# Two of four modulation blocks of the expert layer's norm summed on TensorE instead of VectorE

## The chip, the core and the metric

One core of one Trainium2 chip runs the whole program in one launch. The metric is device time in microseconds (us). TensorE (PE) multiplies matrices, VectorE (DVE) and ScalarE (ACT) work elementwise, GpSimd (POOL) as well, and SyncE (SP) issues transfers. Each engine takes its instructions in order and waits on semaphores.

## The reference, cut to what matters

Two models run one after the other on 256 tokens of width 2048. The first block is

```
mod = silu(c) @ w_ada + b_ada                      # (2048) @ (2048 x 12288)
sh1, sc1, ga1, sh2, sc2, ga2 = split(mod, 6)
h = rmsnorm(x, g_mix) * (1 + sc1) + sh1
x = x + ga1 * hybrid_mixer(h)                      # attention and linear recurrence, then @ w_out
h = rmsnorm(x, g_ffn) * (1 + sc2) + sh2
x = x + ga2 * peer(h)                              # the expert layer
```

and the second model has a state-space layer and an attention layer, each with such a modulation of its own. All is float32. The change touches how `mod` is computed for sh2 and sc2, the modulation of the expert layer's norm.

## The kernel before

A projection goes through tiles of weights: `half` transfers 128 x 1024 weights on SP's queue into `raw`, ScalarE rounds them to `wh` (L352), VectorE subtracts to get the rest `wl` (L354), and TensorE multiplies both by the activations `xs` (L365, L366). Every load calls `tick`, which also advances background work at a rate set per stage.

`mod` is such background work. Its 12288 columns are 12 blocks of 1024: 0 to 3 are sh1 and sc1, 4 and 5 ga1, 6 and 7 sh2, 8 and 9 sc2, 10 and 11 ga2. A block is a vector times 2048 x 1024 weights, in 16 chunks of 128 x 1024 that ScalarE's queue transfers into three buffers `graw` (L281). Two ways exist. With an accumulator (`self.gp` is a pool, as in the whole mixer), VectorE multiplies the first chunk by its 128 factors (L317), adds 15 more (L319) into `gacc`, and TensorE then sums gacc over the partitions with a column of ones (L299), in four column groups of the bank `pg`. Without one (blocks 0 to 3 at the start, 10 and 11 in the expert layer), TensorE takes each chunk itself at L299, four fp32 matmuls with the factors as 32 equal stationary columns, and sums in `pg`. In both, ScalarE copies `pg` (L334), TensorE transposes the copy (L339), and VectorE adds the bias (L341).

There is one bank `pg` and one tile `gacc`. A block is written as a generator: one step for a chunk, then for an accumulator one step each for the sum of columns, the copy and the transposes. The steps of the last chunk, of the sum and of the copy yield PAUSE, which ends a load's share:

```
while self.owed >= 1 and self.bg and self.bg[0][0] != self.hold:
    self.owed -= 1
    if self.advance() == PAUSE:
        break
```

In the mixer the order of loads is w_q, w_k, w_f, w_v (1.5 steps a load), w_lx, w_ly (3 steps a load), then w_out, at a pace that lets the blocks 6 to 9 ("ffn") end within 14 loads (`pace("ffn", 14)`); what is left is done behind the last load (`need("ffn")`). By this count block 6 belongs to the lx loads and the first ly loads, block 7 to the ly loads, block 8 to loads 3 to 8 of w_out, and block 9 to loads 11 to 15 and behind.

Each engine's queue is not simply in the order of the program: the framework orders it by the program's order among what its own model takes for ready, so work may be pulled ahead.

The mixer ends with two norms, of the attention half and of the recurrent half: sums of squares (L441, L445, L451), the reciprocal root (L458 to L471, twelve short VectorE operations in a chain), and per tile L479, L481, L482, which write `xs`. w_out's first five tiles run their first halves on the attention half and their second halves on the recurrent half. The residual is L430. The expert layer's norm comes next (`rstd` again, then L479, L484, L485).

Of the kernel before, what the change touches and what calls it, by code (L numbers as in the profile page):

```python
# [9 lines left out]
F = mybir.dt.float32  # L10
# [138 lines left out]
class K:  # L149
# [131 lines left out]
            self.nc.scalar.dma_start(raw, src)  # L281
            self.ahead.append(raw)

    def gemv(self, w, blocks, which, bias, out, big=False):
        nc = self.nc
        if not big:
            self.chunks += [w[128 * k:128 * k + 128, 1024 * b:1024 * b + 1024] for b in blocks for k in range(KD)]
        return self._gemv(w, blocks, which, bias, out, big)

    def _gemv(self, w, blocks, which, bias, out, big):  # L290
        nc = self.nc
        for b in blocks:
            pg = self.pg()[:, :T]
            c0 = slice(1024 * b, 1024 * b + 1024)
            acc = None if big or self.gp is None else self.gp.tile([128, 1024], F, name="gacc", tag="gacc", bufs=1)

            def columns(lhs, m, start, stop):
                for j in range(4):
                    nc.tensor.matmul(pg[32 * j:32 * j + 32, :], lhs, m[:, T * j:T * j + T], start=start, stop=stop,  # L299
                                     skip_group_check=True, tile_position=(0, 32 * j))  # L300

            for k in range(KD):
                if not big:
                    while not self.ahead:
                        self.fetch_chunk()
                    raw = self.ahead.pop(0)
                else:
                    if k % 4 == 0:
                        rt = self.xs(F).rearrange("p a b t -> p (a b t)").rearrange("p (a c) -> p a c", a=4)
                        self.loads.append(  # L310
                            nc.sync.dma_start(rt, w[128 * k:128 * k + 512, c0].rearrange("(a p) c -> p a c", a=4)))
                    raw = rt[:, k % 4]
                ck = self.cact[:, 16 * which + k:16 * which + k + 1]
                if acc is None:
                    columns(ck.to_broadcast([128, 32]), raw, k == 0, k == KD - 1)
                elif k == 0:
                    nc.vector.tensor_scalar(acc, raw, ck, None, op0=OP.mult)  # L317
                else:
                    nc.vector.scalar_tensor_tensor(acc, raw, ck, acc, op0=OP.mult, op1=OP.add)  # L319
                if not big:  # L320
                    while len(self.ahead) < DEEP and self.chunks:
                        self.fetch_chunk()
                if k < KD - 1:
                    yield True


            if acc is not None:
                if not big:
                    yield PAUSE
                columns(self.ones[:, :32], acc, True, True)  # L330
            if not big:
                yield PAUSE
            ev = self.s1()
            nc.scalar.copy(ev, pg)  # L334
            if not big:
                yield PAUSE
            pm = self.pm()
            for h in range(2):
                nc.tensor.transpose(pm[:, 128 * h:128 * h + 128], ev[:, 128 * h:128 * h + 128], self.ident)  # L339
            v = lambda m: m[:, 8 * b:8 * b + 8].rearrange("p (j h) -> p h j", h=2)  # L340
            nc.vector.tensor_add(v(out), pm[:, :T].rearrange("p (h r) -> p h r", h=2)[:, :, 0:128:32], v(bias))  # L341
            yield False
# [229 lines left out]
    def _mixer(self, x):  # L572
        nc, A, sb, cp = self.nc, self.A, self.sb, self.cp
        mod, hs = self.mod, self.hs
        bias = self.col("b_ada", 0, 96)
        self.use_pool(self.ph if GP[0] else None)
        for n, b in (("ga1", (4, 5)), ("ffn", range(6, 10)), ("ga2", (10, 11))):
            self.bg.append([n, self.gemv(A["w_ada"], b, 0, bias, mod), 19 * len(b) + 1])
        for n, w, nb in (("m0", "mod_w0", 6), ("mkv", "kv_mod_w", 4), ("m1", "mod_w1", 6)):
            t = cp.tile([128, 8 * nb], F, name=n)  # L580
            setattr(self, n, t)
# [1083 lines left out]
```

## Time and profile before

| | |
|---|---|
| median of 3 runs | 3511.92 us (3503.63 to 3515.0) |
| the profiled execution | 3513.32 us, span 3511.6 us |
| TensorE busy | 3220.8 us, 92% of the span |
| VectorE busy | 2688.9 us, 77% |
| ScalarE busy | 1675.5 us, 48% |
| VectorE, multiply-adds of L319 | 429.7 us in 315 instructions, mean 1364 ns |
| TensorE, L299 | 36.8 us in the start, 29.7 us on graw, 14.2 us on gacc |

The mixer runs from about 118 to 552 us of the span. Times in the timelines are from the span's start. "idle before" and a bracket with an arrow name what ended an idle time. A busy TensorE is not TensorE at its peak: matmuls overlap and their ends are modelled.

### The profile page before, as it was taken

How to read it: one execution, taken by the hardware profiler on the slowest of the kernel's cores; microseconds unless marked ns; L12 is line 12 of the kernel's file. 1: busy time of each engine (PE TensorE's matmuls, PEld its weight loads, DVE VectorE, ACT ScalarE, POOL GpSimd, SP SyncE). 2: the span in 40 equal slices, each digit the busy share in tenths (PEclk: the TensorE clock that was granted, in tenths of full speed). 3: DMA queues.
4: the chain of work that ended last, by engine and by line, in shares of the span. 5: the costliest groups of instructions: out<-in, count | busy, mean ns of one | idle time of the engine just before them, and what ended most of it. 6: DMA issues, size and time to landing. Idle time of an engine off the chain costs nothing.

```text
span 3511.6 us, 50080 instructions
## 1 busy us (share of the span) xinstructions
PE 3220.8 (92%) x18190; PEld 2684.6 (76%) x18190; DVE 2688.9 (77%) x4213; ACT 1675.5 (48%) x2785; POOL 841.4 (24%) x750
## 2 busy tenths in 40 slices
PE   5889778999989999999999999988889799999998
PEld 3777667788867878778888778767778688888887
DVE  6778878997668888897777787599996756666665
ACT  3436434456545555444444443455445335555553
POOL 1000211145412212112222630235442120222221
PEclk8999889999989999999999999989999899999999
DMA  9995666567788888888788988545466655444443
GB/s 392 336 344 204 217 235 236 176 238 274 259 279 299 296 278 292 298 287 300 267 289 279 320 298 287 178 146 169 141 219 212 208 194 196 157 149 157 153 145 135
DMA packets 263431, 837.68 MB, mean 239 GB/s; under 512 B 26384, under 2 KB 69520, under 8 KB 260112
## 3 DMA queue, kind: packets, MB, share of 16 engines
q1 hardware_dynamic: 198512, 604.69, 49.9%
q10 hardware_dynamic: 64672, 229.80, 18.0%
q8 instruction: 143, 2.34, 0.3%
q14 instruction: 104, 0.85, 0.1%
HBM read 799.66 MB, written 33.69 MB: 237 GB/s over the span
## 4 chain that ended last, share of the span: by engine, by line
PE 60%; DVE 16%; DMA 12%; issue 5%; POOL 4%; ACT 2%; ACTq 0%; DVEq 0%; SPq 0%; POOLq 0%
PE p L365 25%; PE p L366 13%; DVE wl L354 6%; PE pm L948 5%; PE pm L949 5%; PE pm L950 5%; DMA graw<-mod_w 4%; DVE gacc L319 3%; DMA graw<-w_ada 3%; PE pm L902 1%; DMA graw<-kv_mod_w 1%; DVE xs L1329 1%; PE pg L299 1%; POOL t L929 1%; ACT wh L352 1%
## 5 line engine op out<-in xcount | busy, mean ns | idle before, releaser
L365 PE MATMUL p<-xs,wh 128*128 128x512 f32 x5600 | 2040.0, 406 | 86.5 <-DVE xs L485 44.1
L366 PE MATMUL p<-xs,wl 128*128 128x256 f32 x5600 | 1597.2, 285 | 36.7 <-DVE wl L354 36.4
L354 DVE TENSOR_TENSOR wl<-raw,wh 128x1024 fp32r<-128x1024 f32 x996 | 1262.5, 1274 | 454.7 <-ACT wh L352 452.8
L352 ACT CAST wh<-raw 128x1024 fp32r<-128x1024 f32 x996 | 1039.3, 1049 | 945.8 <-PE p L365 379.1
L365 PEld LDWEIGHTS p<-xs,wh 128*128 128x128 f32 x5600 | 1072.4, 192 | 354.0 <-issue 53.3
L366 PEld LDWEIGHTS p<-xs,wl 128*128 128x128 f32 x5600 | 1077.3, 192 | 60.7 <-DVE wl L354 51.3
L319 DVE SCALAR_TENSOR_TENSOR gacc<-graw,cact,gacc 128x1024 f32<-128x1024 f32 x315 | 429.7, 1364 | 106.1 <-DMA graw<-mod_w 52.9
L949 PE MATMUL pm<-wl,xs 128*128 128x512 f32 x1024 | 400.1, 391 | 4.1 <-DVE wl L354 4.1
L948 PE MATMUL pm<-wh,xs 128*128 128x512 f32 x1024 | 401.8, 392 | 0.5 <-DVE x L958 0.5
L950 PE MATMUL pm<-wh,xs 128*128 128x512 f32 x1024 | 399.0, 390 | 0.0
L933 POOL TENSOR_TENSOR xs<-t,xs 128x256 fp32r<-128x256 f32 x128 | 164.5, 1318 | 715.6 <-ACT xs L931 715.6
L949 PEld LDWEIGHTS pm<-wl,xs 128*128 128x128 f32 x1024 | 192.3, 188 | 46.9 <-DVE wl L354 8.6
L948 PEld LDWEIGHTS pm<-wh,xs 128*128 128x128 f32 x1024 | 192.2, 188 | 45.7 <-issue 6.3
L950 PEld LDWEIGHTS pm<-wh,xs 128*128 128x128 f32 x1024 | 192.2, 188 | 40.0
L929 POOL TENSOR_TENSOR t<-t,t 128x256 f32<-128x256 f32 x128 | 158.6, 1275 | 154.6 <-DMA t<-wd 150.5
L445 POOL TENSOR_TENSOR ssq<-ssq,s 128x256 f32<-128x256 f32 x96 | 101.9, 1071 | 367.1 <-ACT s L441 366.1
L918 ACT ACTIVATE t<-et 128x256 f32<-128x256 f32 x128 | 53.7, 420 | 253.6 <-DVE et L422 249.7
L421 ACT COPY et<-p 128x256 f32<-128x256 f32 x281 | 102.8, 367 | 82.2 <-PE p L366 77.6
L892 POOL TENSOR_SCALAR xs<-iof,eT,eT 128x128 f32<-128x128 f32 x64 | 104.2, 1637 | 110.4 <-PE pm L902 76.7
L1578 POOL TENSOR_SCALAR t<-t,st 128x128 f32<-128x128 f32 (+1 forms) x64 | 78.5, 1239 | 127.4 <-DVE st L1576 124.3
L422 DVE TENSOR_TENSOR et<-p,et 128x256 f32<-128x256 f32 x224 | 92.7, 414 | 10.7 <-ACT et L421 10.7
L1329 DVE TENSOR_TENSOR_SCAN xs<-rho,xs 128x128 f32<-128x128 f32 x128 | 80.0, 678 | 4.3 <-POOL xs L1320 4.3
(388 smaller groups left out, 2872.4 us busy)
## 6 DMA issues: line engine op xcount, KB each, us to landing
raw<-peer_u SPq DMA_DIRECT2D x256, 512.0 KB, 5.6
raw<-peer_v SPq DMA_DIRECT2D x256, 512.0 KB, 4.9
graw<-mod_w ACTq DMA_DIRECT2D x192, 512.0 KB, 6.2
graw<-w_ada ACTq DMA_DIRECT2D x128, 512.0 KB, 5.7
raw<-nsa_z SPq DMA_DIRECT2D x96, 512.0 KB, 3.7
xs<-w_ada SPq DMA_DIRECT2D x16, 2048.0 KB, 13.6
graw<-kv_mod_w ACTq DMA_DIRECT2D x64, 512.0 KB, 6.2
raw<-w_out SPq DMA_DIRECT2D x32, 512.0 KB, 4.8
```

Of the source, the lines that this page charges most:

```text
L319: nc.vector.scalar_tensor_tensor(acc, raw, ck, acc, op0=OP.mult, op1=OP.add)
L352: nc.scalar.copy(h, s)
L354: nc.vector.tensor_sub(l, s, h.bitcast(F))
L365: self.nc.tensor.matmul(p, h[:, sl], x, start=k == 0, stop=False, skip_group_check=True)
L366: self.nc.tensor.matmul(p[:, 1], l[:, sl], x[:, 0], start=False, stop=k == KD - 1, skip_group_check=True)
L892: (nc.gpsimd if j == 3 else nc.vector).tensor_scalar(o[:, 1, j], self.iof, eT[1][:, t + j:t + j + 1], eT[2][:, t + j:t + j + 1], op0=OP.is ...
L929: nc.gpsimd.tensor_mul(gc, gc, wv[:, c])
L933: nc.gpsimd.tensor_sub(ap[:, c - 2, 1], gs[:, c - 2], ap[:, c - 2, 0].bitcast(F))
L948: nc.tensor.matmul(pp[t], ah, h[:, sl], start=c == 0, stop=False, skip_group_check=True)
L949: nc.tensor.matmul(pp[t], ah, l[:, sl], start=False, stop=False, skip_group_check=True)
L950: nc.tensor.matmul(pp[t], ap[:, c, 1, 128 * t:128 * t + 128], h[:, sl], start=False, stop=c == 7, skip_group_check=True)
L1329: nc.vector.tensor_tensor_scan(ma[:, j, i], self.rho[:, g:g + 1].to_broadcast([128, 128]), ma[:, j, i], initial=0.0, op0=OP.mult, op1=OP.add)
```

## The change

`gemv` takes a list `pe` of blocks that get no accumulator. The three calls for w_ada in the mixer pass (6, 8). So blocks 6 and 8, the first half of sh2 and the first half of sc2, go chunk by chunk through L299 on TensorE in the mixer; blocks 4, 5, 7 and 9 stay with VectorE, and 10 and 11 are as before.

```
-    def gemv(self, w, blocks, which, bias, out, big=False):
+    def gemv(self, w, blocks, which, bias, out, big=False, pe=()):
...
-        return self._gemv(w, blocks, which, bias, out, big)
+        return self._gemv(w, blocks, which, bias, out, big, pe)
...
-            acc = None if big or self.gp is None else self.gp.tile([128, 1024], F, name="gacc", tag="gacc", bufs=1)
+            acc = None if big or self.gp is None or b in pe else self.gp.tile([128, 1024], F, name="gacc", tag="gacc", bufs=1)
...
         for n, b in (("ga1", (4, 5)), ("ffn", range(6, 10)), ("ga2", (10, 11))):
-            self.bg.append([n, self.gemv(A["w_ada"], b, 0, bias, mod), 19 * len(b) + 1])
+            self.bg.append([n, self.gemv(A["w_ada"], b, 0, bias, mod, pe=(6, 8)), 19 * len(b) + 1])
```

## Rows read from the trace of the kernel before

**Rows 1.** The page, busy time of each engine.
```profile
PE 3220.8 (92%) x18190; PEld 2684.6 (76%) x18190; DVE 2688.9 (77%) x4213; ACT 1675.5 (48%) x2785; POOL 841.4 (24%) x750
```
**Rows 2.** Busy time by stretch: length, engines, PE clock, DMA share, GB/s.
```profile
268.00:345.00 77.00, 71.28 (x386) 61.28 (x386) 65.67 (x139) 47.47 (x107) 7.02 (x14) 0.96 0.58 205
345.00:422.00 77.00, 56.96 (x288) 45.63 (x287) 64.18 (x112) 36.57 (x76) 14.16 (x11) 0.87 0.61 214
422.00:464.00 42.00, 16.88 (x84) 14.13 (x84) 36.82 (x56) 10.00 (x19) 3.99 (x2) 0.70 0.75 257
464.00:504.00 40.00, 39.96 (x218) 34.37 (x218) 26.63 (x41) 18.16 (x27) 8.23 (x7) 0.93 0.41 147
```
**Rows 3.** Timeline of TensorE, 440 to 465 and 544 to 556: start, length, instruction.
```profile
464.04 0.80 PE L365 MATMUL p<-xs,wh 128*128 128x512 f32 x1 [23.62 <-DVE xs L482]
...
547.90 0.86 PE L299 MATMUL pg<-gacc,ones 128*32 128x256 f32 x8 [3.76 <-DVE gacc L319]
...
552.21 1.06 PE L451 MATMUL pm<-ssq,ones 128*128 128x256 f32 x2
```
**Rows 4.** Timeline of VectorE, 425 to 463.
```profile
426.72 1.27 DVE L319 SCALAR_TENSOR_TENSOR gacc<-graw,cact,gacc 128x1024 f32<-128x1024 f32 x1
...
437.86 2.68 DVE L319 SCALAR_TENSOR_TENSOR gacc<-graw,cact,gacc 128x1024 f32<-128x1024 f32 x2
...
441.59 0.42 DVE L458 TENSOR_SCALAR s<-pm 128x256 f32<-128x256 f32 x1
...
443.70 1.22 DVE L354 TENSOR_TENSOR wl<-raw,wh 128x1024 fp32r<-128x1024 f32 x1
...
461.44 0.42 DVE L471 SCALAR_TENSOR_TENSOR rstd<-s,rstd 128x256 f32<-128x256 f32 x1
```
**Rows 5.** Timeline of VectorE, 542 to 560.
```profile
554.23 0.42 DVE L458 TENSOR_SCALAR s<-pm 128x256 f32<-128x256 f32 x1 [1.40 <-PE pm L451]
...
559.16 0.42 DVE L471 SCALAR_TENSOR_TENSOR rstd<-s,rstd 128x256 f32<-128x256 f32 x1
```
**Rows 6.** Busy time by stretch, L319 alone: one stretch for each block 6 to 9.
```profile
243.00:292.00 49.00, 19.02 (x15) 0.97 0.90 321
349.00:407.00 58.00, 19.70 (x15) 0.88 0.60 209
418.00:462.00 44.00, 19.22 (x15) 0.70 0.76 269
504.00:548.00 44.00, 20.72 (x15) 1.00 0.94 335
```
**Rows 7.** Timelines of ScalarE and TensorE at the bank pg.
```profile
291.30 0.35 ACT L334 COPY s<-pg 128x256 f32<-128x256 f32 x1
...
406.97 0.64 PE L299 MATMUL pg<-gacc,ones 128*32 128x256 f32 x8 [1.15 <-DVE gacc L319]
...
466.52 0.37 ACT L334 COPY s<-pg 128x256 f32<-128x256 f32 x1
```
**Rows 8.** Timeline of TensorE in the next stage, one chunk and three chunks.
```profile
706.42 0.28 PE L366 MATMUL p<-xs,wl 128*128 128x256 f32 x1
...
707.20 0.50 PE L365 MATMUL p<-xs,wh 128*128 128x512 f32 x1
...
992.79 0.28 PE L366 MATMUL p<-xs,wl 128*128 128x256 f32 x1
993.00 1.50 PE L299 MATMUL pg<-graw,cact 128*32 128x256 f32 x24
994.43 0.50 PE L365 MATMUL p<-xs,wh 128*128 128x512 f32 x1
```
**Rows 9.** Who waited for whom, 200 to 345: total us, times, longest.
```profile
DVE gacc L319 <- DMA graw<-w_ada: 14.6, 10, 3.1
PE pm L750 <- DVE sl L744: 2.9, 2, 2.6
```
**Rows 10.** Who waited for whom, 430 to 470.
```profile
DVE gacc L319 <- DMA graw<-w_ada: 3.6, 5, 1.0
```

More of the change, by code (lines that the diff above doesn't have):

```diff
@@ L287, in gemv, with _gemv @@
             self.chunks += [w[128 * k:128 * k + 128, 1024 * b:1024 * b + 1024] for b in blocks for k in range(KD)]
-        return self._gemv(w, blocks, which, bias, out, big)
-    def _gemv(self, w, blocks, which, bias, out, big):
+        return self._gemv(w, blocks, which, bias, out, big, pe)
+    def _gemv(self, w, blocks, which, bias, out, big, pe):
         nc = self.nc
```

## Prediction

> **What bounds the kernel now.** I read the totals first, then the stretches of the mixer, then TensorE's longest waits there, then VectorE's timeline at the longest.
>
> TensorE is the busiest engine of the whole run, VectorE second [rows 1]. That average hides the place of this change. In the stretches of the mixer [rows 2] TensorE is nearly full while the lx columns run (71.28 of 77 us from 268 to 345) and full in the first part of the output projection (39.96 of 40 us from 464 to 504). Between them it is not: it idles 20.0 us of the 77 from 345 to 422, and 25.1 us of the 42 from 422 to 464, where VectorE is busy for 36.82 us. The reader is to see that a microsecond of work costs TensorE a microsecond in the first two stretches, and that VectorE sets the pace in the other two.
>
> The 25 us are nearly all one wait: TensorE stands 23.62 us, until 464.04, for the second half of the mixer's normed rows (xs, L482) [rows 3]. VectorE's timeline shows why [rows 4]. The reciprocal root that comes ahead of L482 takes from 441.59 (L458) to 461.86 us (last L471), 20.3 us, because its twelve short operations alternate with the 1.28 us multiply-adds of block 8 (L319). The same chain ahead of the expert layer, with nothing between, takes from 554.23 to 559.58 us, 5.35 us [rows 5]. All 15 multiply-adds of block 8 fall between 418 and 462, where they cost 19.22 us [rows 6]. In the program they belong to the projection's loads 3 to 8: the framework has pulled them ahead into what it took for VectorE's free time.
>
> **The change, part by part.**
>
> *Removed from VectorE:* the 15 multiply-adds of block 6 between 243 and 292, 19.02 us, and those of block 8, 19.22 us [rows 6]; the first multiply of each block is not counted. Also removed, from TensorE: one sum of columns over gacc per block, 0.64 us [rows 7].
>
> *Added to TensorE:* 16 chunks a block, each four fp32 matmuls of 128x32 with 256 columns (eight records). The trace has them in the next stage. One chunk alone moves the next L365 from 0.12 us after the last L366 (an estimate from the steps where nothing stands between) to 0.78 us (706.42 to 707.20): 0.66 us. Three together move it to 1.64 us (992.79 to 994.43): 1.52 us [rows 8]. At three steps a load, block 6 comes as two, four threes, two, and block 8 as five threes and one: 8.3 us each, taking a pair as 1.09. Less 0.64 for the sum that goes, 7.7 us each. Bounds: 16 times 0.51 less 0.64, 7.5; 16 times 0.66 less 0.64, 9.9.
>
> The Trainium skill (TensorEngine Tiling (Array Packing), Tiling Modes, Key Properties) says that a change of tiling mode drains TensorE. The rows agree in that a lone chunk costs 0.66 and one in company 0.51. If every chunk came alone, the two blocks would cost 19.8 us by that, not 15.4.
>
> *Where block 6 goes.* Its columns need the bank pg. That is free only when ScalarE has copied block 5's sum out, at 291.30 [rows 7], while the multiply-adds of before had a tile of their own and ran from 243. So the columns run in the lx stretch, where TensorE has little idle time: +7.7. What VectorE gains there is worth little: of the waits from 200 to 345, 2.9 us are TensorE's for an attention head's softmax (L744) [rows 9]; I take 2 back (bounds 0 and 2.9). TensorE now stands in order for each chunk's transfer. VectorE stood 14.6 us for them in that stretch [rows 9], for block 5 as well and where the DMA was fuller; the bounds are 0 and 7.3, half of it. I take 1, since the DMA share is only 0.58 from 268 on [rows 2]. Block 6: +6.7.
>
> *Where block 8 goes.* For the same reason it waits for the copy of block 7's sum. Before, that sum is made at 406.97, yet ScalarE copies it only at 466.52, among the casts of the norm [rows 7]. So block 8's columns come behind that norm, in the full stretch: +7.7. Waits for chunks: VectorE stood 3.6 us for them [rows 10]; between 0 and 3.6 I take 2. What is queued behind such a wait on TensorE is the next projection tile, and behind a late release of a graw buffer ScalarE's next chunk transfer, which ScalarE issues in order ahead of its casts.
>
> *What it frees.* In the chain from 441.59 there remain 5.35 us [rows 5] and one 1.22 us subtraction of wl that stands there too [rows 4]: 6.6 instead of 20.3, so -13.7. Ahead of it, from 426.72 to 440.54, six more multiply-adds (first and last in [rows 4], 7.7 us) stand between the last tile's gelu and L458: -7.7. Together -21.4, within the wait of 23.62; TensorE ends the five first halves at 440.4 and would go on about 2 us later. What is late next is then the norm itself, as before. Bounds: 13.7 and 23.6.
>
> *Pacing.* A block on TensorE has one step fewer, a pause that ends a load's share. By counting the steps, block 7 moves one load ahead, and block 9 two: its last chunk goes from behind the last load to the second last. In the stretch with 20.0 us of idle I take 2 for block 7's earlier end (bounds 0 and 10). At the mixer's end TensorE is done at 544.14, waits 3.76 us for block 9's last chunk, makes its sum, and begins the sum of squares at 552.21 [rows 3]. Without block 9 in the way some 2 us are left of these 8.1 (last residual, square): up to -6. I take 4, since block 9 now follows block 8 through the same three buffers (bounds 0 and 6).
>
> *Nothing else.* Blocks 4, 5, 10 and 11 are not in (6, 8); bytes, transfers and copies stay the same in number. SP's queue is not touched. The accumulator is free of 6 and 8, which alone would let 7 and 9 begin sooner.
>
> **The sum:** 6.7 + 7.7 + 2 - 21.4 - 2 - 4 = -11.0 us against the profiled execution's 3513.3, which makes 3502.3. That execution is 1.4 us above the median of 3511.9 (runs from 3503.6 to 3515.0), so the median comes to 3501.
>
> **The rivals.**
>
> *More comes back (3487).* The 20.0 us of idle from 345 to 422 are VectorE's doing too, which is busy for 64.18 us there [rows 2]. If block 7, a load earlier, frees half of them (-10 instead of -2), the tail gives its 6 and the chunk waits are 0, the sum is -11 - 8 - 2 - 3 = -24: about 3487. Against: block 7 itself stays with VectorE in that very stretch.
>
> *The waits move along (3509).* TensorE takes over VectorE's waits for chunks, 7.3 and 3.6 instead of 1 and 2: +7.9, so 3509. For it: an in-order queue either way. Against: the DMA share is lower where the columns now run, 0.58 and 0.41 [rows 2].
>
> *The chunk stream becomes the bound (3533).* Blocks 8 and 9, 32 chunks, must now both follow the copy of block 7's sum, through three buffers. I place that copy at 447 (466.5 less 21.4, and some 2 for the norm) and add 7 for block 6: 454. At block 9's pace of before, 2.75 us a chunk (16 in 44 us), they end at 542, sooner than the sum at 547.90 of before; at block 7's pace, 3.6 us (16 in 58 us) [rows 6], at 569, 21 us later: 3533. It decides from 2.9 us a chunk up. For it: before, block 8 had run ahead during the wait. Against: only 147 GB/s are drawn from 464 to 504 [rows 2], so the new transfers have room. This is the rival that ends slower.
>
> *Full price, nothing back (3527).* If other work fills VectorE's chain, the wait stays and the columns cost 15.4: 3527. The candidate is block 9, whose accumulator is free; against it, its chunks queue behind block 8's, which wait for the copy. The Trainium skill (Perfetto Trace Analysis, Identifying the Most-Contended Engine) says to improve the engine with the highest occupancy first; by that, loading TensorE [rows 1] is wrong, where the stretches have VectorE as the busy one from 422 to 464 [rows 2].
>
> That the change does nothing is excluded: the mixer has a pool, so both blocks had an accumulator before.
>
> **How the numbers follow.** About 0.3%, 10.5 us, is what a measurement of this kernel can tell from no change. Forecast 0.36, its centre just at that bound (0.19 faster, 0.17 same); more comes back 0.26; waits move along 0.19; stream 0.13; full price 0.06. So faster 0.45, same 0.36, slower 0.19. The range runs from 3483, below the largest gain, to 3527, the full price; what it leaves out is the slow stream and a little below. The likeliest case's own range is 3494 to 3509.
>
> **What would show it.** Right: L458 to the last L471 of the mixer's second norm in 7 us or less, TensorE's wait for L482 under 5 us, block 6's columns after ScalarE's copy of block 5 and block 8's after that of block 7, 8 to 10 us of displacement each, the sum of squares within 3 us of the last matmul on w_out. Wrong: multiply-adds of block 9 inside that chain, TensorE idle ahead of L299 for graw by more than 5 us, block 9's last chunk still behind the last load, or block 8's columns found inside the old wait.

## The result, and the profile after

The changed kernel takes 3531.76 us (median of five runs, 3527.28 to 3538.18), the kernel before beside it 3511.01 us: a ratio of 1.0061, with a 95% interval of [1.0048, 1.0074]. It is 0.6% slower, where 3501 us was forecast. The profiled execution took 3527.28 us, with a span of 3525.6 us.

The page's busy times, which answer to [rows 1]:

```profile
PE 3246.7 (92%) x18430; PEld 2696.4 (76%) x18430; DVE 2653.8 (75%) x4181; ACT 1681.4 (48%) x2789; POOL 847.3 (24%) x750
```

VectorE has 35 us less to do and TensorE 26 us more; the page says no more than that. The stretches of [rows 2], with the projection's second part as a fifth row:

```profile
268.00:345.00 77.00, 74.28 (x476) 57.18 (x475) 51.95 (x115) 42.94 (x97) 6.66 (x13) 0.98 0.63 207
345.00:422.00 77.00, 57.13 (x269) 46.28 (x267) 55.11 (x87) 35.38 (x72) 15.98 (x11) 0.84 0.62 206
422.00:464.00 42.00, 29.04 (x153) 23.32 (x152) 35.97 (x79) 17.56 (x34) 1.74 (x2) 0.84 0.41 134
464.00:504.00 40.00, 37.30 (x270) 27.42 (x269) 17.66 (x23) 12.64 (x17) 4.41 (x5) 1.00 0.83 293
504.00:552.00 48.00, 42.71 (x235) 35.40 (x234) 42.28 (x47) 18.66 (x24) 10.50 (x8) 1.00 0.94 343
```

From 422 to 464 TensorE has 29.04 us of work in place of 16.88: the gap ahead of the projection is smaller. From 345 to 422 it still idles 19.9 us, although VectorE has 9 us less to do there. And from 464 to 504 the DMA share is 0.83, where it was 0.41: block 8's chunks now come beside the projection's weights.

TensorE's timeline, which answers to [rows 3] and to the bank's rows in [rows 7]: the first and last columns of block 6, block 7's sum, the second norm, the first and last columns of block 8, block 9's sum, the end of w_out.

```profile
289.08 1.07 PE L299 MATMUL pg<-graw,cact 128*32 128x256 f32 x16
...
344.11 0.63 PE L299 MATMUL pg<-graw,cact 128*32 128x256 f32 x6
...
414.54 1.08 PE L299 MATMUL pg<-gacc,ones 128*32 128x256 f32 x8 [5.46 <-DVE gacc L319]
...
457.67 0.79 PE L365 MATMUL p<-xs,wh 128*128 128x512 f32 x1 [6.72 <-DVE xs L482]
...
462.10 1.50 PE L299 MATMUL pg<-graw,cact 128*32 128x256 f32 x24
...
500.27 0.64 PE L299 MATMUL pg<-graw,cact 128*32 128x256 f32 x8
...
544.79 0.62 PE L299 MATMUL pg<-gacc,ones 128*32 128x256 f32 x2
...
559.97 0.28 PE L366 MATMUL p<-xs,wl 128*128 128x256 f32 x1
...
562.39 0.60 PE L451 MATMUL pm<-ssq,ones 128*128 128x256 f32 x2
```

VectorE's chain of the second norm, which answers to [rows 4]:

```profile
449.65 0.42 DVE L458 TENSOR_SCALAR s<-pm 128x256 f32<-128x256 f32 x1
...
452.03 1.22 DVE L354 TENSOR_TENSOR wl<-raw,wh 128x1024 fp32r<-128x1024 f32 x1
...
455.46 0.43 DVE L471 SCALAR_TENSOR_TENSOR rstd<-s,rstd 128x256 f32<-128x256 f32 x1
```

The chain takes 6.2 us in place of 20.3, with the one subtraction of wl that was left in it, and TensorE's wait for L482 is 6.72 us in place of 23.62. The step that the prediction put most on is as it said. But the wait ends at 457.67, only 6.4 us sooner than before, because all ahead of it is late: block 7's sum is made at 414.54 behind a wait of 5.46 us, where it was made at 406.97 behind 1.15 [rows 7].

Matching the matmuls of the weights (L365) one by one gives how far each trace is behind that of before, in us, at the places where before stood at these times. A row is the first matmul of an output tile, the last one the first of the next stage. The columns behind the first two are experiments told below; the last of them has the same program as before up to 562 us, so that its column shows what chance does to such a number: up to 6 us to its level, but at most 1.5 from one row to the next.

```
before at   the change   pauses kept   block 6's columns left out   same mixer
   316         -0.3         -1.7                1.8                    -4.7
   328          8.6          7.2                2.3                    -6.2
   363         15.8          0.2                2.3                    -4.9
   405         18.5          1.6              -10.3                    -3.8
   431         13.2          0.1              -12.7                    -4.3
   470         -1.2        -16.2              -29.9                    -2.9
   498          8.6         -3.9              -10.6                    -3.2
   538         16.0         -3.4               -3.8                    -3.5
   562          9.3         -5.0               -9.6                    -4.4
```

Read down the changed kernel's column (in steps from row to row): +9 while block 6's columns end in lx (expected, 6.7), 5 to 10 more in ly (a gain of 2 was expected), a large gain at the norm, +10 for block 8's columns (expected, 7.7 and 2), another 7 in the projection's second part (not expected), and back some 7 at the end (4 was expected). The mixer ends 9 us late. The two profiled executions differ by 14.0 us and the medians by 21, so that by the medians about 12 more are lost behind it, where the prediction had nothing; the experiments below test that.

### The profile page after: what moved, and what is told of

The parts are those of the page before. It is cut to its first block, busy times and chain, and to the rows that moved or that the text cites. A ratio compares the mean times of both kernels' runs of the same rounds, so it can differ in the third digit from the quotient of the medians.

```text
span 3525.6 us, 50448 instructions
## 1 busy us (share of the span) xinstructions
PE 3246.7 (92%) x18430; PEld 2696.4 (76%) x18430; DVE 2653.8 (75%) x4181; ACT 1681.4 (48%) x2789; POOL 847.3 (24%) x750
## 4 chain that ended last, share of the span: by engine, by line
PE 60%; DVE 17%; DMA 12%; issue 6%; POOL 2%; ACT 2%; ACTq 0%; DVEq 0%; SPq 0%; POOLq 0%
PE p L365 24%; PE p L366 12%; DVE wl L354 6%; PE pm L948 5%; PE pm L950 5%; PE pm L949 5%; DMA graw<-mod_w 4%; DVE gacc L319 3%; DMA graw<-w_ada 2%; DMA graw<-kv_mod_w 2%; PE pm L902 1%; PE pg L299 1%; DMA s5d<-tb 1%; DVE xs L1329 1%; ACT wh L352 1%
## 5 line engine op out<-in xcount | busy, mean ns | idle before, releaser
L365 PE MATMUL p<-xs,wh 128*128 128x512 f32 x5600 | 2044.5, 407 | 69.2 <-DVE xs L485 44.6
L366 PE MATMUL p<-xs,wl 128*128 128x256 f32 x5600 | 1599.9, 286 | 45.4 <-DVE wl L354 45.0
L365 PEld LDWEIGHTS p<-xs,wh 128*128 128x128 f32 x5600 | 1072.8, 192 | 341.2 <-issue 57.9
L366 PEld LDWEIGHTS p<-xs,wl 128*128 128x128 f32 x5600 | 1079.6, 193 | 73.2 <-DVE wl L354 63.4
L319 DVE SCALAR_TENSOR_TENSOR gacc<-graw,cact,gacc 128x1024 f32<-128x1024 f32 x285 | 393.2, 1379 | 112.6 <-DMA graw<-mod_w 57.2
L948 PE MATMUL pm<-wh,xs 128*128 128x512 f32 x1024 | 401.1, 392 | 3.7 <-DVE x L958 3.7
L949 PE MATMUL pm<-wl,xs 128*128 128x512 f32 x1024 | 398.7, 389 | 0.0
L948 PEld LDWEIGHTS pm<-wh,xs 128*128 128x128 f32 x1024 | 192.2, 188 | 49.5 <-issue 6.3
L949 PEld LDWEIGHTS pm<-wl,xs 128*128 128x128 f32 x1024 | 192.3, 188 | 39.0
L929 POOL TENSOR_TENSOR t<-t,t 128x256 f32<-128x256 f32 x128 | 166.4, 1333 | 168.4 <-DMA t<-wd 165.1
```

What stands on the lines that cost most here:

```text
L365: self.nc.tensor.matmul(p, h[:, sl], x, start=k == 0, stop=False, skip_group_check=True)
L366: self.nc.tensor.matmul(p[:, 1], l[:, sl], x[:, 0], start=False, stop=k == KD - 1, skip_group_check=True)
L929: nc.gpsimd.tensor_mul(gc, gc, wv[:, c])
L948: nc.tensor.matmul(pp[t], ah, h[:, sl], start=c == 0, stop=False, skip_group_check=True)
L949: nc.tensor.matmul(pp[t], ah, l[:, sl], start=False, stop=False, skip_group_check=True)
```

## The experiments

Sixteen kernels ran. Ratios are to the kernel before, run beside each on the same chip (3511.0 to 3512.9 us), with 95% intervals. Where a fragment of a line is shown, the rest of it is unchanged.

**One block at a time.** Two theories stood at first: each block costs or gains what its own stretch has to give (a full stretch in lx, a gap ahead of w_out), or each costs some 10 us through pace or queues, wherever it stands.

```diff
-  pe=(6, 8)
+  pe=(6,)        # and (7,), (8,), (9,)
```

Block 6 alone. 

> Only block 6 goes to TensorE. Stretch theory (a block on TensorE costs what TensorE has no idle time for, and gives back only what VectorE's chain made TensorE wait): from the two traces the lag at the projection's tiles grows by 10 us through the lx columns and by another 5 to 12 through the ly columns, and the old 23.6 us wait with block 8's multiply-adds stays, so 14 to 20 us slower than before, 3525 to 3531. Rival (every block that leaves VectorE shifts the pacing and the chunk queue alike, whichever it is): half of the whole change, 10 us slower, 3521.

Block 7 alone. 

> Only block 7 goes to TensorE; its chunks fall in the ly columns, where TensorE idles 20 us before. Stretch theory: the columns fit into idle time and VectorE's waits for chunks no longer hold up the weights' rests, so 0 to 10 us faster than before, 3501 to 3511. Rival (pacing and chunk queue): 10 us slower, 3521, with TensorE itself idle ahead of L299 for chunk transfers.

Block 8 alone. 

> Only block 8 goes to TensorE. Stretch theory: the lag falls by 22 us where the second norm's wait was, rises by 10 with the columns in the projection, rises by up to 7 where block 9's multiply-adds come close behind, and falls by 6 at the mixer's end: 8 to 14 us faster than before, 3497 to 3503. Rival (pacing and chunk queue): 10 us slower, 3521.

Block 9 alone. 

> Only block 9 goes to TensorE; its chunks fall in the projection's second part, where TensorE is full, and the second norm's wait with block 8 stays. Stretch theory: 10 us for the columns less up to 6 at the mixer's end, so 2 to 8 us slower than before, 3513 to 3519. Rival (pacing and chunk queue): 10 us slower, 3521.

Measured: block 6 3536.09 us, 1.0077 [1.0057, 1.0096]; block 7 3519.98 us, 1.0026 [1.0009, 1.0042]; block 8 3521.32 us, 1.0030 [1.0015, 1.0046]; block 9 3525.88 us, 1.0047 [1.0032, 1.0061]. All four are slower, and neither theory holds. Blocks 7 and 8 came close to the 3521 of the second, but 8 was to gain by the first; block 6 cost more than either said, and 9 cost more than the first said and a little more than the second. The traces held the clue. Block 7's mixer ended 6.6 us earlier than that of before, and the run was still 9 us slower. Only block 9's loss was complete at the mixer's end.

Counting the steps of the program gives a reason. A block on TensorE has a PAUSE fewer, and the steps owed at the mixer's end are kept while the background is on hold, up to a cap of 1. Before, the last load of w_out leaves 0.54 (7.5/14); with block 6, 7 or 8 on TensorE, the last load ends on another pause, more than 1 is owed, and the cap leaves 1.00. With block 9 alone it stays 0.54. The remainder goes into the expert layer, where the pace is 1.25 and then 1.23 steps a load, and shifts the later modulations by one weight load: by the count, 19 steps of the first 40 loads come one load sooner, and 239 of the 250 behind them one load later.

**The expert layer's phase alone.**

```diff
-        self.need("ffn")
+        self.need("ffn"); self.owed = 1.0       # in the kernel before
+        self.need("ffn"); self.owed = 7.5 / 14  # in kernels with blocks on TensorE
```

The kernel before, entering at 1.0: 

> The kernel before, all four blocks on VectorE; after the mixer the steps that are owed to the background are set to 1.0, the value at which the changed kernel enters the expert layer (the kernel before enters it with 0.54). The mixer stays as it is; in the expert layer each background step of the later modulations falls one weight load later, in exactly the changed kernel's order. Theory 'phase of the expert layer': this order alone costs 8 to 16 us, 3519 to 3527 us, and the profile falls behind the one before only after 562 us. Rival 'all of the loss is made in the mixer': 3509 to 3513 us.

Measured: 3526.68 us, 1.0045 [1.0027, 1.0062]. Not one instruction was moved between engines, and it lost 15 us.

The changed kernel, entering at 0.54: 

> The changed kernel with the owed steps set back to 0.54 after the mixer: its mixer, and behind it the instruction order of the kernel before. Theory 'phase of the expert layer': what is left is the mixer's own +9 us, 3517 to 3524 us. Rival 'all of the loss is made in the mixer': 3530 to 3534 us, as the changed kernel.

Measured: 3520.24 us, 1.0026 [1.0011, 1.0040]: 11.5 us less than the changed kernel, and still 8.4 above before.

Block 7 alone, entering at 0.54: 

> Block 7 alone on TensorE, and the owed steps set back to 0.54 after the mixer. Its mixer ended 6.7 us earlier than that of the kernel before. Theory 'phase of the expert layer': 3502 to 3508 us, faster than the kernel before. Rival 'all of the loss is made in the mixer' (the lag in one profile was chance): 3518 to 3522 us, as block 7 alone was.

Measured: 3502.48 us, 0.9972 [0.9958, 0.9986]. With the phase of before, a block on TensorE gains.

Blocks 7 and 8, entering at 0.54: 

> Blocks 7 and 8 on TensorE in place of 6 and 8, the owed steps set back to 0.54 after the mixer. Theory 'phase of the expert layer', with block 7's 6.7 us gained in ly and block 8's columns paid by the closed wait of the second norm: 3500 to 3508 us. Rival 'each block on TensorE costs about 10 us wherever it stands': 3528 to 3532 us. Third case, that block 9 behind block 8 again holds up the weights in the projection by 6 to 8 us: 3508 to 3514 us.

Measured: 3493.61 us, 0.9953 [0.9937, 0.9970], 38 us below the changed kernel with as many blocks on TensorE.

The first three lie in the range that the theory of the phase gave; the fourth is 6 us faster than its range, so that the swap of blocks 7 and 8 gave more than was put down for it. In the traces its size is read from the last L471 of the norm ahead of the expert layer to the last L948 of the expert layer. Timelines of VectorE and TensorE in the kernel before (its last L471 is in [rows 5]), in the kernel before entering at 1.0, in the changed kernel, and in the changed kernel entering at 0.54:

```profile
2272.90 0.39 PE L948 MATMUL pm<-wh,xs 128*128 128x512 f32 x1
```

```profile
554.77 0.43 DVE L471 SCALAR_TENSOR_TENSOR rstd<-s,rstd 128x256 f32<-128x256 f32 x1
...
2280.49 0.39 PE L948 MATMUL pm<-wh,xs 128*128 128x512 f32 x1
```

```profile
568.47 0.43 DVE L471 SCALAR_TENSOR_TENSOR rstd<-s,rstd 128x256 f32<-128x256 f32 x1
...
2283.54 0.39 PE L948 MATMUL pm<-wh,xs 128*128 128x512 f32 x1
```

```profile
563.07 0.42 DVE L471 SCALAR_TENSOR_TENSOR rstd<-s,rstd 128x256 f32<-128x256 f32 x1
...
2270.16 0.39 PE L948 MATMUL pm<-wh,xs 128*128 128x512 f32 x1
```

That makes 1713.7, 1725.7, 1715.1 and 1707.1 us. The 13 kernels that enter at 0.54 take 1705.4 to 1713.7 us for this stretch (mean 1709), the five that enter at 1.00 1715.0 to 1725.7 (mean 1720): the groups do not overlap, and their means are 10 us apart. One pair of profiles would not have shown it: those of before and after differ by 1.4. TensorE's granted clock goes with it: the stretch holds 1670 us at the upper of its two levels (2.4 GHz) in the mean of either group (1664 to 1678), and at the lower (1.2 GHz) 39.7 us in the mean of the thirteen (33.2 to 46.2) and 49.9 us in that of the five (36.8 to 61.4). Whether longer waits brought the clock down or the lower clock made the stretch longer, no run separates.

Where the 10 us arise is not one wait. Who waited for whom from 700 to 2310, in the kernel before:

```profile
PE pm L872 <- DVE e L862: 0.7, 1, 0.7
...
PE pm L948 <- DVE x L958: 0.5, 1, 0.5
```

and in the kernel before entering at 1.0:

```profile
PE pm L948 <- DVE x L958: 4.7, 3, 2.2
PE pm L872 <- DVE e L862: 3.5, 2, 2.7
```

These two grew by 7.0 us together, and the same two are longer in the changed kernel (3.7 and 3.6); the waits for wl at L366, the largest, are equal (32.4 and 32.7). Others became shorter (wl at L949 from 4.1 to 0.8), so that all of TensorE's waits in this view grew by 5.3 us, not by 12. The rest was not traced to a place.

**The pauses in the mixer.**

```diff
-            if acc is not None:
-                if not big:
-                    yield PAUSE
-                columns(self.ones[:, :32], acc, True, True)
+            if (acc is not None or b in pe) and not big:
+                yield PAUSE
+            if acc is not None:
+                columns(self.ones[:, :32], acc, True, True)
```

> Blocks 6 and 8 on TensorE as in the change, but each keeps the pause that the change drops with the accumulator's sum, so that every other step of the mixer and all behind it is issued at the same place as in the kernel before. Theory 'the slip in ly is one of pacing' (block 7's steps, moved one load forward, fall badly): TensorE's wait for block 7's sum, 5 to 6 us in the changed kernel, falls to about 1, the second norm's stretch begins 5 to 8 us earlier than in the changed kernel, and the whole takes 3509 to 3516 us. Rival 'the slip comes with the swap of engines' (block 6's columns delay the chunks that block 7 needs): the wait stays, 3517 to 3524 us, as with the owed steps set back alone.

Measured: 3505.37 us, 0.9985 [0.9972, 0.9998]. The same two blocks stand on TensorE, and it is 26 us faster than the changed kernel. It is more than was expected, 3509 to 3516 us: the +7 in lx is gone again in ly (0.2 at 363 us, some 5 up to 376, and -0.5 to -0.8 from 387 to 396).

Who waited for whom from 336 to 440, first in the kernel before, for VectorE and for TensorE:

```profile
DVE gacc L319 <- DMA graw<-w_ada: 8.4, 5, 3.2
...
PE p L366 <- DVE wl L354: 3.1, 2, 2.6
...
PE pg L299 <- DVE gacc L319: 1.2, 1, 1.2
```

in the changed kernel:

```profile
DVE gacc L319 <- DMA graw<-w_ada: 14.1, 4, 6.0
...
PE p L366 <- DVE wl L354: 6.6, 2, 5.1
...
PE pg L299 <- DVE gacc L319: 5.5, 1, 5.5
```

and with the pauses kept:

```profile
DVE gacc L319 <- DMA graw<-w_ada: 2.0, 2, 1.1
...
PE pg L299 <- DVE gacc L319: 1.1, 1, 1.1
```

The timelines of VectorE and TensorE in the changed kernel show how these waits hang together:

```profile
391.17 1.28 DVE L319 SCALAR_TENSOR_TENSOR gacc<-graw,cact,gacc 128x1024 f32<-128x1024 f32 x1 [3.63 <-DMA graw<-w_ada]
...
411.35 1.28 DVE L319 SCALAR_TENSOR_TENSOR gacc<-graw,cact,gacc 128x1024 f32<-128x1024 f32 x1 [6.04 <-DMA graw<-w_ada]
```

```profile
395.17 0.58 PE L366 MATMUL p<-xs,wl 128*128 128x256 f32 x1 [5.10 <-DVE wl L354]
```

With the pauses kept, TensorE's timeline at block 7's sum and at the second norm:

```profile
408.51 0.64 PE L299 MATMUL pg<-gacc,ones 128*32 128x256 f32 x8 [1.11 <-DVE gacc L319]
...
445.26 0.80 PE L365 MATMUL p<-xs,wh 128*128 128x512 f32 x1 [4.94 <-DVE xs L482]
```

VectorE takes its queue in order: while block 7's multiply-add stands for a chunk, what is queued behind it stands too. Behind the 3.63 us until 391.17 it is a low half of weights, for which TensorE waits until 395.17; behind the 6.04 us until 411.35 it is the end of block 7, for whose sum TensorE waits until 414.54. With block 7's steps one load later VectorE stands 2.0 us in all, and the sum is made at 408.51. Why these chunks came late is not shown; TensorE's last columns of block 6 begin at 344.11, so that of the four stands only the first, 3.52 us until 353.30, can lie directly behind them.

**Block 6's columns left out.**

```diff
-                    columns(ck.to_broadcast([128, 32]), raw, k == 0, k == KD - 1)
+                    (b != 6 or k % 15 == 0) and columns(ck.to_broadcast([128, 32]), raw, k == 0, k == KD - 1)
```

> The changed kernel with the owed steps set back after the mixer (3520 us), in which block 6's columns are left out but for its first and its last chunk: 56 of 64 matmuls, 9.2 us of TensorE. Block 6's sums are then not those of the reference. Theory 'TensorE is full in lx and pays the columns in full': 3509 to 3513 us, and the lag at 336 us falls from 8 to about 0. Rival 'the columns lie in cover and the lag comes from the re-pacing of lx': 3518 to 3522 us.

Measured: 3494.50 us, 0.9950 [0.9934, 0.9967]: 26 us less than with the columns (the changed kernel entering at 0.54), not 9. Both theories fall short. The lag at 328 us falls by 5 (7.5 to 2.3), so that lx does pay for the columns; but the slip in ly goes as well, although the steps of the program stand where they stood. VectorE's waits for chunks from 336 to 440 in this kernel:

```profile
DVE gacc L319 <- DMA graw<-w_ada: 3.6, 2, 2.4
```

Does the slip then need both, block 7's steps one load forward and block 6's columns on TensorE? This run does not settle it, for the steps stand still only in the program. VectorE's first product of block 7, in this kernel and then in the changed one:

```profile
288.93 0.73 DVE L317 TENSOR_SCALAR gacc<-graw,cact 128x1024 f32<-128x1024 f32 x1
```

```profile
340.95 0.75 DVE L317 TENSOR_SCALAR gacc<-graw,cact 128x1024 f32<-128x1024 f32 x1 [0.52 <-DMA graw<-w_ada]
```

Without block 6's columns block 7 begins 52 us sooner, its sum is made at 401.20 in place of 414.54, and block 8's first columns run at 433.09 in place of 462.10. So more than the columns' own time went with the edit. What the run shows is that with block 7's chunks fetched that early the slip does not come.

**Block 9 behind block 8.**

```diff
-                else:
+                elif big or out is not self.mod or b != 9 or k == KD - 1:
                     nc.vector.scalar_tensor_tensor(acc, raw, ck, acc, op0=OP.mult, op1=OP.add)
```

> The changed kernel with the owed steps set back after the mixer (3520 us), in which block 9's multiply-adds are left out but for the first product and the last multiply-add: 14 instructions, 18 us of VectorE. Block 9's sums are then not those of the reference; its chunks are still loaded. Theory 'block 9 right behind block 8 holds up the low halves of the weights': the waits for wl in the projection go, 3511 to 3515 us. Rival 'the loads themselves pace the projection': the waits stay, 3518 to 3522 us.

Measured: 3515.31 us, 1.0015 [1.0001, 1.0029], 5 us less, with intervals that overlap, and just above the range of the one theory and below that of the other. The projection's second part and TensorE's waits from 460 to 552 in the changed kernel entering at 0.54:

```profile
504.00:552.00 48.00, 43.56 (x243) 35.81 (x242) 41.54 (x46) 18.34 (x25) 10.35 (x9) 1.00 0.95 348
```

```profile
PE p L366 <- DVE wl L354: 4.4, 5, 1.4
PE pg L299 <- DMA graw<-w_ada: 2.5, 3, 1.2
```

The stretches of the projection and the same waits without block 9's multiply-adds:

```profile
464.00:504.00 40.00, 35.23 (x240) 24.55 (x240) 17.31 (x23) 12.01 (x16) 4.40 (x5) 0.91 0.79 275
504.00:552.00 48.00, 45.60 (x266) 39.25 (x265) 27.68 (x35) 18.92 (x25) 6.74 (x8) 1.00 0.97 353
```

```profile
PE pg L299 <- DMA graw<-w_ada: 4.7, 4, 1.4
PE p L366 <- DVE wl L354: 2.4, 2, 1.5
```

VectorE has 14 us less to do from 504 to 552, and TensorE's waits are 7.1 us still (6.9 with the multiply-adds). By the waits for wl, the theory that I had formed from the trace, that the multiply-adds hold up the weights, explains 2 us (4.4 to 2.4). Matched as in the table, the loss from 498 to 538 falls by 4 (6.3 to 2.3), but the first part, where the granted clock is 0.91 in place of 1.00, loses 5 more. How much of the 7 us is the multiply-adds' stays open. The DMA share does not explain the rest: with the pauses kept, the same stretch loses next to nothing at a share just as high (498 to 538 in that kernel):

```profile
498.00:538.00 40.00, 38.89 (x223) 33.65 (x221) 37.24 (x42) 15.02 (x21) 10.08 (x7) 1.00 0.97 355
```

From 498 to 538 the lag grows by 7.4 us in the changed kernel and by 0.5 with its pauses kept; with block 8 alone by 10.7 and 0.4, with blocks 7 and 8 by 6.2 and 0.1 (the kernels with kept pauses are told below). So the loss there, too, goes with the moved steps, block 9 close behind block 8.

The projection's steps over 16 loads, in the version with blocks 7 and 8:

```diff
-        self.pace("ffn", 14)
+        self.pace("ffn", 16)
```

> Blocks 7 and 8 on TensorE with the owed steps set back (3494 us), and the steps of the projection spread over 16 weight loads in place of 14. Theory 'block 9's multiply-adds come too densely': the waits for wl in the projection fall from some 7 to 3 us or less, 3488 to 3492 us. Rival 'the chunk stream or the tail takes it back' (block 9 ends later, and what is left is forced behind the last matmul): 3493 to 3500 us.

Measured: 3498.36 us, 0.9961 [0.9946, 0.9976]: no gain. The waits for wl fell as the theory said (6.0 us to 2.4, from 460 to 552), but the time lies in the rival's range.

**Each block's price with its pause kept.** The edit is that of the pauses above, with the blocks named.

Block 6. 

> Block 6 alone on TensorE, its pause kept (without it: 3536 us). Theory 'the dropped pause': its 9 us of lag in lx come back in ly, the wait for the second norm stays, 3508 to 3516 us. Rival 'the columns cost it': only the expert layer's 12 us come back, 3521 to 3527 us.

Block 8. 

> Block 8 alone on TensorE, its pause kept (without it: 3521 us, of which 12 in the expert layer). Theory 'the dropped pause': the second norm's wait closes by some 20 us, the columns take back 10 to 14, and block 9, one weight load later, no longer holds up the projection: 3497 to 3506 us. Rival 'the columns and block 9 take the gain whatever the pace': 3508 to 3513 us.

Block 9. 

> Block 9 alone on TensorE, its pause kept (without it: 3526 us). Block 9 is the last of the mixer's blocks, so that its dropped pause moves no step of another block and leaves the expert layer as it was. Theory 'the dropped pause' therefore expects no change here: 3522 to 3529 us, the columns in the projection being the price. Rival 'a kept pause helps whatever block it belongs to': 3509 to 3518 us.

Blocks 7 and 8. 

> Blocks 7 and 8 on TensorE, both pauses kept (with the pauses dropped and the owed steps set back: 3494 us). Theory 'the dropped pause': block 9 no longer holds up the projection, 3484 to 3492 us. Rival 'block 7 gains from coming one load earlier': 3495 to 3505 us.

| blocks | pause dropped | pause kept |
|---|---|---|
| 6 | 3536.09, 1.0077 | 3513.81, 1.0005 [0.9990, 1.0019] |
| 8 | 3521.32, 1.0030 | 3505.69, 0.9981 [0.9967, 0.9995] |
| 9 | 3525.88, 1.0047 | 3523.63, 1.0034 [1.0020, 1.0048] |
| 7 and 8 | 3493.61, 0.9953 (entering at 0.54) | 3494.96, 0.9950 [0.9932, 0.9968] |

Block 6's loss of 25 us is all but gone, block 8 turns into a gain, and block 9, whose pause moves nothing, stays as it was: so it is the dropped pause in 6 and 8, and the columns in 9. For blocks 7 and 8 the time lies at the edge of the rival's range and 3 us above the theory's: keeping the pauses gives what setting back the owed steps gives, so that here the moved steps cost nothing that can be told.

Block 8 alone shows the projection too. TensorE's waits from 460 to 552 with the pause dropped, and then with it kept:

```profile
PE p L366 <- DVE wl L354: 7.0, 2, 5.4
```

```profile
PE p L366 <- DVE wl L354: 1.6, 1, 1.6
```

The waits for wl are shorter by 5.4 us with the pause kept, those for chunks (3.7 us to 5.2) and for the copy of pg (1.6 to 4.2) longer by 4.1 together.

## Why the prediction was wrong

The loss of 21 us (1.0061 of 3512) falls into three parts, each by what an experiment gave back: about 12 us by the phase of the expert layer (1.0061 to 1.0026), about 14 us by the moved steps in the mixer (1.0026 to 0.9985), and a gain of about 5 us (0.9985, interval 1 to 10) by the swap of engines itself.

1. *Pacing* is the step that failed. It saw that a block on TensorE has one pause fewer and that block 7 moves one load ahead and block 9 two, and it priced that as a gain of 2 in ly. It cost about 14 us in the mixer. Moving a block earlier was taken to end it earlier; but block 7's sum was made 7.6 us later than before (414.54 in place of 406.97), since its multiply-adds stood 14.1 us for transfers in place of 8.4, with TensorE's weights and the sum behind them. With the steps back in their places they stood 2.0 us. What delays the chunks is open.
2. *Nothing else* failed as well, by 12 us. It counted the blocks, the bytes and the queues, not the state that the pacer carries out of the mixer. The bounds of the sum held no term for it; with the remainder set to 1.0 alone, the kernel before loses 15 us.
3. *Block 6, +6.7*: it stands 9 us late at 328, and leaving out most of its columns takes away 5 there, so the columns cost no more than the 7.7 taken (the edit takes with them their waits for chunks, 2.7 us where I took 1). What comes back was undersized: with the pauses kept, all 7 are gone by 387, where I took 2. That it is VectorE's gain is argued, not shown.
4. *The second norm, -21.4*: the mechanism is right, and the wait itself gave 16.9 (23.62 to 6.72), 18.7 with the pauses kept, where 4.94 us of it are left. The sum took some 3 to 5 too much: it left 2.2 of the wait, though TensorE, with its five first halves done, waits for the norm longer than that.
5. *Block 8, +7.7 and 2*: 9.8 from 470 to 498, as predicted; then 7 more to 538 that no term held. The DMA share there, 0.94 before and after, is not the reason, since with the pauses kept the loss is 0.5 at 0.97. It is *Pacing* again: block 9's two loads forward, which I counted as a gain at the tail, bring it close behind block 8.
6. *The tail, -4*: 6.7 back between 538 and 562. Block 9's sum is made at 544.79 with no wait, and the sum of squares begins 2.1 us after the end of the last matmul on w_out, as predicted.

Without its two terms for pacing (-2 and -4) the sum is -5.0, beside a measured gain of 5.3 with the pauses kept. That is partly luck, since block 6 came cheaper and the norm's wait gave less.

Of the rivals, the chunk stream (3533) came nearest in time, but not by its mechanism: block 9's 16 chunks took from 498.95 to 542 us, 2.7 us each, under the 2.9 from which it was to decide, and the projection lost 7 us, not 21. Of the signs, the chain (6.2 us of 7), the order behind ScalarE's copies (285.06 and 459.89, the columns at 289.08 and 462.10) and the sum of squares (2.1 us of 3) came as for *right*; the wait for L482, 6.72 us, did not, and TensorE's waits for chunks, 2.7 us in each block's stretch, make 5.4 where more than 5 was to mean *wrong*. *More comes back* did not happen in the changed kernel; block 7's 10 us of ly are what block 7 itself on TensorE gains (lag -9.5 at 431 with blocks 7 and 8 there).

The Trainium skill (Perfetto Trace Analysis, Identifying the Most-Contended Engine) says to improve the most occupied engine first, but to judge TensorE by the share of its peak that its matmuls reach or by the time of its weight loads, not by its busy matmuls. The prediction took the 92% of the matmuls and called the change wrong by that rule; by the weight loads TensorE stands at 76%, beside VectorE's 77% [rows 1], so that the rule speaks against neither. The runs do not bear out a full TensorE as the cause: with the pauses kept, more work on TensorE made the program faster, by 0.15% with blocks 6 and 8 and by 0.50% with 7 and 8.

What stays open: why block 7's chunks come late when its steps move one load forward, what makes up the 10 to 15 us of the expert layer, beyond waits that grew by 5 us in all and 10 us more at the lower clock, and whether another phase than 0.54 would be better still.

## What to carry to other kernels

Where a change drops a step from work that is paced by counting steps, follow the count to the end of the program: the remainder that the pacer carries on is part of the change, and here it and the moved steps cost some 26 us, where the swap gave 5. To test a swap of engines, keep the steps (an empty pause will do), so that all else is issued where it was; then re-pace on its own. And where a transfer feeds an engine that takes its queue in order, ask whether the transfers will have landed at the new time before calling "earlier" a gain.

## What the runs showed of the hardware

The order of a few off-path instructions by one weight load, with the same work on the same engines, is worth 15 us in 3512 (1.0045). The projection's second part moves 335 to 355 GB/s at a DMA share of 0.94 to 0.97, in kernels that lose 7 us there and in one that loses 0.5, so that so high a share did not by itself slow the matmuls; and 14 us less of VectorE's work there changed TensorE's waits by 0.2 us. And two profiles of one and the same mixer ended 4.4 us apart (559.16 [rows 5] and 554.77), so that a few us are not read from one pair of traces.
